# First tile of x in two halves with its norm weights beside it, first weight columns first on their queue, five warm-up matmuls for nine

## The chip, the cores and the metric

The kernel runs on one core of one Trainium2 chip. The metric is the device time of one execution in microseconds (us); the figure given for a kernel is the median of its runs. Before the change it is 734.75 us, the median of three runs that lie between 734.32 and 734.83.

## What is computed

One block of a hybrid model on 512 tokens of width 1024, in 32-bit floats. Each row of x is normalised (RMS) and scaled by g_mix, and one wide projection w_in makes the inputs of two branches, a gated linear attention in two directions and a latent attention with a rotary part. Their outputs are mixed by two sigmoid gates, projected by w_out and added to x. A feed-forward part with a squared ReLU and a last normalisation follow. Cut to what bears on this change:

```python
def reference(x, ...):
    n = rmsnorm(h, g_mix[l])          # x * rsqrt(mean(x*x) + EPS) * g_mix
    proj = n @ w_in[l]
    (gq, gk, gv, gr, z_gf, z_gb, cq, ckv, kr, z_ma, z_mb) = jnp.split(proj, SPLIT_IDX, axis=-1)
    y_gla = gla_branch(gq, gk, gv, gr, ...)
    y_mla = mla_branch(cq, ckv, kr, ...)
    merged = jax.nn.sigmoid(z_ma) * y_gla + jax.nn.sigmoid(z_mb) * y_mla
    h = h + merged @ w_out[l]
    m = rmsnorm(h, g_mlp[l])
    h = h + jnp.square(jax.nn.relu(m @ w_ff1[l])) @ w_ff2[l]
    return rmsnorm(h, g_final)
```

The change touches only the start of `n @ w_in`: the first 128 of the 1024 features of x, against the first 512 columns that the kernel wants of w_in.

## The kernel before

**Arithmetic.** x is handed in transposed (`xt`, features by tokens), so that it lies in eight tiles of 128 features by 512 tokens, k = 0 to 7. A 32-bit product is made of three products of a shorter format: each operand is split into a high part (a rounding copy) and a low part (what is left), and high by high, low by high and high by low are summed in PSUM. The factor 1/rms of a row is not known at the start; the products are made with x times g_mix alone, and 1/rms is multiplied in later.

**The start.** Four column groups of 128 (the query and key of head 0 and two groups of the gate z_mb) are gathered on the host into `w_first`, 1024 by 512. TensorE (PE) sums all four side by side in four PSUM banks, `f_accs[0]` to `f_accs[3]`: for each k three groups of four matmuls of 128x512 (`first_with(k)`), 12 per tile and 96 in all. In the trace the tiles of x are `x`, the loaded weights `vw`, the split x is `xT` (high part and low part in one tile), the split weights are `first0h`, `first0l` and so on (two k to a tile), and the banks are `first`.

**What feeds it.** SyncE (SP) issues the loads of x and of the weights in turn, tile by tile; ScalarE (ACT) issues two: `gvec`, which holds all norm weights and biases as columns (g_mix among them), and columns 128 to 511 of the first weight tile. Each engine works through its own list in order; a DMA that finds its turn of the eight completion counters still in use waits for the load eight places before it. For k = 0, VectorE (DVE) makes the high part of the weights in two casts (128 and 384 columns), ACT makes the high part of x (`ACTIVATE xT<-x,gvec`, scaled by the column of g_mix), and DVE then makes the two low parts. For k > 0 both high parts are ACT's. ACT also squares each tile of x for 1/rms.

**Before the data is there** PE runs nine matmuls of ones by ones into a bank of no use (`warm`). Each is in 32-bit floats and shows as two rows in the trace.

**What sets the order.** The start is written in program order, and each engine is held to it. From `nc.keep()` to `nc.flush((0.0, TABLES))` the rest of the kernel is collected and put in order by a planner (`Due`) from costs and due times that it works out itself.

Nearly every instruction passes through `Script.lay`, so that it shows as L233, and rows are told apart by their tiles. The loads stand at L732 to L741, the warm-ups at L745, `first_with` at L751, and the splitting of each tile at L768 to L784.

Of the kernel before, what the change touches and what calls it, by code (L numbers as in the profile page):

```python
# [13 lines left out]
F32R = mybir.dt.float32r  # L14
I32 = mybir.dt.int32
AF = mybir.ActivationFunctionType
ALU = mybir.AluOpType
AX = mybir.AxisListType

P = 128  # L20
S = 512
NT = S // P
D = 1024
KD = D // P
# [436 lines left out]
def tile_block(ctx: ExitStack, tc: tile.TileContext, t, out: bass.AP):  # L461
# [7 lines left out]
    bass_nc, nc = tc.nc, Script(tc.nc, issued_after)  # L469
# [5 lines left out]
    def tl(shape, dt, tag, bufs, name):  # L475
        serial[0] += 1
        name = f"{name}_{serial[0]}"
        return hold(lambda: sb.tile(shape, dt, tag=tag, bufs=bufs, name=name), shape, dt, tag, bufs, name)

    def hold(make, shape, dt, tag, bufs, name):  # L480
        h = Held(make, shape, dt, tag, bufs)
        h.name = name
        if nc.kept is None:
            nc.takes(h)
        return View.whole(h)

    def u2(name, dt=F32, shape=(P, S)):
        return tl(list(shape), dt, "u2", 24, name)

    def u4(name, dt=F32R, shape=(P, 2, S)):  # L490
        return tl(list(shape), dt, "u4", 30, name)
# [4 lines left out]
    def ps(tag, name):  # L496
        serial[0] += 1
        name = f"{name}_{serial[0]}"
        return hold(lambda: pp.tile([P, S], F32, tag=tag, bufs=4, name=name), [P, S], F32, tag, 4, name)

    def one(shape, dt, name):
        return hold(lambda: sb.tile(shape, dt, tag=name, bufs=1, name=name), shape, dt, name, None, name)

    def raw(x):
        return x.bitcast(F32)
# [6 lines left out]
    def split(hi, lo, src, rest=nc.vector):  # L512
        nc.scalar.activation(hi, src, AF.Copy)
        rest.tensor_tensor(lo, src, raw(hi), op=ALU.subtract)

    def split_scaled(hi, lo, src, scale):
        nc.scalar.activation(hi, src, AF.Copy, scale=scale)
        nc.vector.scalar_tensor_tensor(lo, src, scale, raw(hi), op0=ALU.mult, op1=ALU.subtract)

    def traced():  # L520
        return len(nc.cur_bb.bb.instructions)
# [25 lines left out]
    TABLES = {AF.Exp: 1, AF.Tanh: 1, AF.Ln: 2, AF.Sin: 3}  # L547
    V_GLA, V_Q, V_KV, V_MLP, V_BF, V_BB, V_MIX, V_CST = 0, 8, 11, 13, 21, 25, 29, 37
    gvec = one([P, 48], F32, "gvec")
    nc.scalar.dma_start(gvec[:, 0 : V_CST + 2], t["columns"])  # L550
    ident = one([P, P], F32, "ident")
    make_identity(bass_nc, ident.real())
    after = one([P, P], F32, "after")
# [4 lines left out]
    ones = one([P, P], F32, "ones")  # L558
    nc.vector.memset(ones, 1.0)
    ones_r = one([P, P], F32R, "ones_r")  # L560
    nc.vector.tensor_copy(ones_r, ones)
    half_pi = one([P, 1], F32, "half_pi")
    nc.gpsimd.memset(half_pi, float(np.pi / 2))
    mhalf = one([P, 1], F32, "mhalf")
# [5 lines left out]
    gmix, cst = gvec[:, V_MIX : V_MIX + 8], gvec[:, V_CST : V_CST + 2]  # L570
# [70 lines left out]
    def halves(nk, nw, name):  # L641
        wh = tl([P, nk, nw], F32R, "wh", 4, f"{name}h")
        wl = tl([P, nk, nw], F32R, "wl", 4, f"{name}l")
        return wh, wl
# [86 lines left out]
    xT = [u4(f"xT{k}") for k in range(KD)]  # L731
    xraw = [u2(f"x{k}") for k in range(KD)]  # L732
    vraw = [u2(f"vw{k}") for k in range(KD)]

    landing = traced()
    for k in range(KD):
        nc.sync.dma_start(xraw[k], t["xt"][k * P : (k + 1) * P, :])
        parts = ((nc.sync, slice(0, S)),) if k else ((nc.sync, slice(0, P)), (nc.scalar, slice(P, S)))
        for queue, c in parts:
            queue.dma_start(vraw[k][:, c], t["w_first"][k * P : (k + 1) * P, c])  # L740

    landing = landing, traced()
    fixed = traced()
    warm = ps("at", "warm")
    for _ in range(9):  # L745
        nc.tensor.matmul(warm[:, :P], ones, ones, start=True, stop=True)
    f_accs = [ps("mm", f"first{i}") for i in range(NT)]
    vh = [halves(2, S, f"first{k}") for k in range(KD // 2)]
    sq = None

    def first_with(k):  # L751
        hi, lo = xT[k][:, 0, :], xT[k][:, 1, :]
        wh, wl = vh[k // 2][0][:, k % 2, :], vh[k // 2][1][:, k % 2, :]
        for x, (a, b) in enumerate(((wh, hi), (wl, hi), (wh, lo))):
            for i in range(NT):
                nc.tensor.matmul(
                    f_accs[i], a[:, i * P : (i + 1) * P], b, start=k == 0 and x == 0, stop=k == KD - 1 and x == 2
                )

    def add_square(k, before):  # L760
        q = u2(f"sq{k}")
        nc.scalar.activation(q, xraw[k], AF.Square)
        if before is not None:
            nc.vector.tensor_tensor(q, q, before, op=ALU.add)
        return q

    for k in range(KD):
        wh, wl = (vh[k // 2][x][:, k % 2, :] for x in range(2))  # L768
        if k == 0:
            for c in (slice(0, P), slice(P, S)):  # L770
                nc.vector.tensor_copy(wh[:, c], vraw[k][:, c])
            hi, lo = xT[k][:, 0, :], xT[k][:, 1, :]
            nc.scalar.activation(hi, xraw[k], AF.Copy, scale=gmix[:, k : k + 1])
            nc.vector.tensor_tensor(wl, vraw[k], raw(wh), op=ALU.subtract)
            nc.vector.scalar_tensor_tensor(
                lo, xraw[k], gmix[:, k : k + 1], raw(hi), op0=ALU.mult, op1=ALU.subtract
            )
        else:
            split_scaled(xT[k][:, 0, :], xT[k][:, 1, :], xraw[k], gmix[:, k : k + 1])
            split(wh, wl, vraw[k])  # L780
        if k < 6:
            first_with(k)
        if k:
            sq = add_square(k - 1, sq)  # L784
# [7 lines left out]
    for k in range(KD):  # L792
        nc.scalar.activation(xraw[k], xraw[k], AF.Copy, scale=gmix[:, k : k + 1])
    first_with(6)
    first_with(7)
    x_diag = rstd_diag(x_tot, D, "x", False, zb_early[0][1])
    zb_early[1][1]()
# [953 lines left out]
    for n in range(4 * MH + LAG_C - 1):  # L1751
# [9 lines left out]
        b = n - LAG_B  # L1761
# [7 lines left out]
        for x, at in (("y", (18, 26, 34)), ("z", (20, 28, 36))):  # L1769
            if n in at:  # L1770
                p = at.index(n)
                to = (5, 6) if x == "y" else (7, 3)
                split_sum(wo_left[p], sums_of[p, x], *to, f"{x}o{p}", nc.gpsimd if p < 2 else nc.vector)
        if n in (19, 30):
            p = (19, 30).index(n)
# [17 lines left out]
        c = n - LAG_C  # L1793
# [702 lines left out]
def build(arrays):  # L2496
    nc = bacc.Bacc("TRN2", target_bir_lowering=False, num_devices=1, dynamic_dma_scratch_size=8192)
    t = {
        n: nc.dram_tensor(f"in_{n}", list(a.shape), mybir.dt.from_np(a.dtype), kind="ExternalInput").ap()
        for n, a in arrays.items()  # L2500
    }
    out = nc.dram_tensor("out_0", [1, S, D], F32, kind="ExternalOutput").ap()
    with tile.TileContext(nc) as tc:
        tile_block(tc, t, out)
    return nc
# [16 lines left out]
```

## Time and profile before

| What | Value |
|---|---|
| median of three runs | 734.75 us (734.32 to 734.83) |
| the profiled execution, first to last instruction (its span) | 733.0 us |
| mean granted TensorE clock of that execution | 0.998 |
| PE busy | 724.6 us, 99% of the span |
| PE weight loads busy | 635.9 us |
| DVE busy | 608.6 us |
| ACT busy | 515.8 us |
| GpSimd (POOL) busy | 199.8 us |

The profiled execution's own time is given as its span only; the median of the runs is 1.75 us above it. Times in the rows are microseconds from the start of the span. A row of the timeline has start, duration, engine, line, operation, output <- inputs, shapes and a count where like instructions in a row are merged; in square brackets stands how long the engine was idle before and what ended that. ACTq and SPq rows are the issuing of DMAs. Loads have a time from issue to landing of their own. The ends of matmuls are modelled, so their pace is read from start to start.

### The profile page before, as it was taken

To read this page: it belongs to the slowest core of one execution; us is meant where nothing else is said; L and a number is where in the kernel's file an instruction comes from. 1 tells how busy PE (TensorE), PEld (TensorE's weight loads), DVE (VectorE), ACT (ScalarE), POOL (GpSimd) and SP (SyncE) were. 2 spreads that over 40 slices of the span, in tenths; PEclk is the share of its full clock that TensorE was granted. 3 is DMA by queue.
4 is the path that set the end of the run, shared out by engine and by line. 5 is a ranking of instruction groups with operands and counts; after the bars stand their busy time and mean duration, and the time that the engine had idled before them with its cause. 6 is when DMAs were issued, how large, how long until landed. Compare 5 with 4: busy or idle time off the path is not lost.

```text
span 733.0 us, 11354 instructions
## 1 busy us (share of the span) xinstructions
PE 724.6 (99%) x4126; PEld 635.9 (87%) x4126; DVE 608.6 (83%) x960; ACT 515.8 (70%) x863; POOL 199.8 (27%) x207
## 2 busy tenths in 40 slices
PE   9999999999999999999999999999999999999996
PEld 8888888888899888888888999889988998889985
DVE  7694766669999789899998899968895789768885
ACT  8575665669998567998865788737864587458844
POOL 0133040401201215038843231321232212212433
PEclk9999999999999999999999999999999999999999
DMA  9979795742322224239996899898999888998973
GB/s 322 324 152 178 202 204 104 124 107 57 88 59 55 37 54 107 59 111 257 232 288 97 194 208 247 173 196 205 212 217 211 210 192 200 211 226 175 227 146 116
DMA packets 105306, 124.37 MB, mean 170 GB/s; under 512 B 16321, under 2 KB 68801, under 8 KB 105249
## 3 DMA queue, kind: packets, MB, share of 16 engines
q0 software_dynamic: 32992, 51.12, 41.3%
q1 hardware_dynamic: 71824, 72.04, 31.7%
q8 instruction: 32, 0.52, 0.3%
q10 hardware_dynamic: 432, 0.48, 0.2%
q14 instruction: 26, 0.20, 0.1%
HBM read 119.95 MB, written 2.10 MB: 167 GB/s over the span
## 4 chain that ended last, share of the span: by engine, by line
PE 99%; issue 0%; DVE 0%; ACT 0%; POOLq 0%; POOL 0%
PE mb L233 25%; PE ab L233 18%; PE zb L233 4%; PE first L233 3%; PE s L233 3%; PE av L233 3%; PE wox L233 3%; PE gvx L233 3%; PE zax L233 3%; PE grx L233 3%; PE cq L233 2%; PE gq L233 2%; PE gk L233 2%; PE tp L233 2%; PE uv L233 2%; PE ckv L233 1%
## 5 line engine op out<-in xcount | busy, mean ns | idle before, releaser
L233 POOL DMA_DIRECT2D ms<-in_w_ff x37 | 48.0, 1394 | 118.8 <-DVE hl0l L233 40.9
L233 POOL DMA_DIRECT2D w1s<-in_w_ff x19 | 24.3, 1277 | 85.5 <-DVE hl2l L233 25.8
L233 DVE TENSOR_TENSOR h<-h,ab 128x512 f32<-128x512 f32 x48 | 31.6, 681 | 8.4 <-PE ab L233 8.4
L233 ACT ACTIVATE row<-row 128x512 f32<-128x512 f32 x56 | 34.8, 623 | 1.2 <-DVE row L233 0.6
L233 PE MATMUL s<-kbuf,q 96*128 96x512 f32 x96 | 28.7, 409 | 0.0
L233 PE MATMUL av<-pT,v 128*128 128x512 f32 (+1 forms) x108 | 28.3, 383 | 0.0
L233 PE MATMUL mb<-four,hl0h 128*128 128x256 f32 x144 | 26.4, 283 | 0.0
L233 ACT ACTIVATE row<-mb 128x512 f32<-128x512 f32 x30 | 17.7, 589 | 9.5 <-PE mb L233 9.2
L233 ACT ACTIVATE e<-s,top 128x512 f32<-128x512 f32 x32 | 21.9, 685 | 3.4 <-DVE top L233 3.4
L233 PE MATMUL mb<-four,hl3h 128*128 128x256 f32 x128 | 23.5, 283 | 0.0
L233 DVE TENSOR_REDUCE top<-s 128x1 f32<-128x512 f32 x32 | 21.8, 683 | 1.7 <-PE s L233 1.5
L233 PEld LDWEIGHTS mb<-four,hl0h 128*128 128x128 f32 x144 | 22.8, 192 | 0.4
L233 DVE TENSOR_TENSOR pT<-tp,pT 128x512 fp32r<-128x512 f32 x32 | 21.7, 679 | 1.6 <-ACT pT L233 1.3
L233 ACT ACTIVATE pT<-tp 128x512 fp32r<-128x512 f32 x32 | 18.9, 595 | 2.9 <-PE tp L233 2.7
L233 PE MATMUL mb<-four,hl2h 128*128 128x256 f32 x112 | 20.5, 283 | 0.0
L233 PEld LDWEIGHTS mb<-four,hl3h 128*128 128x128 f32 x128 | 20.2, 192 | 0.3
L233 PE MATMUL mb<-four,hl0l 128*128 128x256 f32 x72 | 20.4, 283 | 0.0
L233 PE MATMUL tp<-ident,e 128*128 128x128 f32 x128 | 20.1, 273 | 0.0
L233 PEld LDWEIGHTS av<-pT,v 128*128 128x128 f32 x108 | 17.8, 189 | 2.6
L233 PEld LDWEIGHTS s<-kbuf,q 96*128 96x128 f32 x96 | 16.8, 189 | 3.4 <-ACT e L233 0.7
L233 ACT ACTIVATE hl3h<-ms 128x1024 fp32r<-128x1024 f32 x12 | 12.7, 1057 | 9.7 <-PE ab L233 4.6
L233 PEld LDWEIGHTS tp<-ident,e 128*128 128x128 f32 x128 | 15.8, 140 | 4.0 <-PE tp L233 0.2
(1122 smaller groups left out, 2789.0 us busy)
## 6 DMA issues: line engine op xcount, KB each, us to landing
ms<-in_w_ff POOLq DMA_DIRECT2D x37, 512.0 KB, 7.2
w1s<-in_w_ff POOLq DMA_DIRECT2D x19, 512.0 KB, 7.3
ms<-in_w_ff SPq DMA_DIRECT2D x16, 512.0 KB, 5.6
w1s<-in_w_ff SPq DMA_DIRECT2D x15, 512.0 KB, 6.0
wf0f<-in_w_ff SPq DMA_DIRECT2D x11, 512.0 KB, 6.5
wf1f<-in_w_ff SPq DMA_DIRECT2D x11, 512.0 KB, 5.9
wf2f<-in_w_ff SPq DMA_DIRECT2D x11, 512.0 KB, 6.2
w<-in_w_out POOLq DMA_DIRECT2D x10, 512.0 KB, 8.6
```

The costliest lines, as they stand in the source:

```text
L233: return call(*map(real, work.args), **{k: real(v) for k, v in work.named.items()})
```

## The change

Five edits, all at the start:

1. The first half (tokens 0 to 255) of the first tile of x comes as a new array `x_head`, 128 by 257, whose last column is g_mix of these 128 features. It is the first load on SP's queue. The second half is loaded into the tile of x by the second.
2. The first 128 weight columns move from SP's queue to the front of ACT's, ahead of the other 384; `gvec` goes behind both.
3. For k = 0 the high and the low part of x are each made in two halves, scaled by the column in `x_head` instead of the one in `gvec`. POOL copies the first half into the tile of x, where the squares read it.
4. The first matmul of the first bank becomes two of 256 tokens. So that both may add, the bank is first set by a matmul of `ones_r` with a tile of zeros (`nil`, made by DVE from `ones`).
5. Four matmuls of ones are left; with the one that sets the bank PE has five before the first real one.

The two new tiles come from the pool of 24 that x, weights and others share. The order on every engine behind the start is the same as before.

```diff
@@ -547,7 +547,6 @@
     TABLES = {AF.Exp: 1, AF.Tanh: 1, AF.Ln: 2, AF.Sin: 3}
     V_GLA, V_Q, V_KV, V_MLP, V_BF, V_BB, V_MIX, V_CST = 0, 8, 11, 13, 21, 25, 29, 37
     gvec = one([P, 48], F32, "gvec")
-    nc.scalar.dma_start(gvec[:, 0 : V_CST + 2], t["columns"])
     ident = one([P, P], F32, "ident")
     make_identity(bass_nc, ident.real())
     after = one([P, P], F32, "after")
@@ -559,6 +558,10 @@
     nc.vector.memset(ones, 1.0)
     ones_r = one([P, P], F32R, "ones_r")
     nc.vector.tensor_copy(ones_r, ones)
+    nil = u2("nil", F32R)
+    nc.vector.tensor_scalar(
+        nil.rearrange("p (a b) -> p a b", a=NT), ones.unsqueeze(1).to_broadcast([P, NT, P]), 0.0, None, op0=ALU.mult
+    )
     half_pi = one([P, 1], F32, "half_pi")
     nc.gpsimd.memset(half_pi, float(np.pi / 2))
     mhalf = one([P, 1], F32, "mhalf")
@@ -732,19 +735,26 @@
     xraw = [u2(f"x{k}") for k in range(KD)]
     vraw = [u2(f"vw{k}") for k in range(KD)]
 
+    HEAD = S // 2
+    x_head = u2("x_head")
     landing = traced()
-    for k in range(KD):
+    nc.scalar.dma_start(vraw[0][:, 0:P], t["w_first"][0:P, 0:P])
+    nc.sync.dma_start(x_head[:, 0 : HEAD + 1], t["x_head"])
+    nc.scalar.dma_start(vraw[0][:, P:S], t["w_first"][0:P, P:S])
+    nc.sync.dma_start(xraw[0][:, HEAD:S], t["xt"][0:P, HEAD:S])
+    nc.scalar.dma_start(gvec[:, 0 : V_CST + 2], t["columns"])
+    for k in range(1, KD):
         nc.sync.dma_start(xraw[k], t["xt"][k * P : (k + 1) * P, :])
-        parts = ((nc.sync, slice(0, S)),) if k else ((nc.sync, slice(0, P)), (nc.scalar, slice(P, S)))
-        for queue, c in parts:
-            queue.dma_start(vraw[k][:, c], t["w_first"][k * P : (k + 1) * P, c])
+        nc.sync.dma_start(vraw[k], t["w_first"][k * P : (k + 1) * P, :])
+    nc.gpsimd.tensor_copy(xraw[0][:, 0:HEAD], x_head[:, 0:HEAD])
 
     landing = landing, traced()
     fixed = traced()
     warm = ps("at", "warm")
-    for _ in range(9):
+    for _ in range(4):
         nc.tensor.matmul(warm[:, :P], ones, ones, start=True, stop=True)
     f_accs = [ps("mm", f"first{i}") for i in range(NT)]
+    nc.tensor.matmul(f_accs[0], ones_r, nil, start=True, stop=False)
     vh = [halves(2, S, f"first{k}") for k in range(KD // 2)]
     sq = None
 
@@ -752,7 +762,10 @@
         hi, lo = xT[k][:, 0, :], xT[k][:, 1, :]
         wh, wl = vh[k // 2][0][:, k % 2, :], vh[k // 2][1][:, k % 2, :]
         for x, (a, b) in enumerate(((wh, hi), (wl, hi), (wh, lo))):
-            for i in range(NT):
+            if k == x == 0:
+                for c in (slice(0, HEAD), slice(HEAD, S)):
+                    nc.tensor.matmul(f_accs[0][:, c], a[:, 0:P], b[:, c], start=False, stop=False)
+            for i in range(1 if k == x == 0 else 0, NT):
                 nc.tensor.matmul(
                     f_accs[i], a[:, i * P : (i + 1) * P], b, start=k == 0 and x == 0, stop=k == KD - 1 and x == 2
                 )
@@ -769,12 +782,13 @@
         if k == 0:
             for c in (slice(0, P), slice(P, S)):
                 nc.vector.tensor_copy(wh[:, c], vraw[k][:, c])
-            hi, lo = xT[k][:, 0, :], xT[k][:, 1, :]
-            nc.scalar.activation(hi, xraw[k], AF.Copy, scale=gmix[:, k : k + 1])
+            hi, lo, g = xT[k][:, 0, :], xT[k][:, 1, :], x_head[:, HEAD : HEAD + 1]
+            parts = (slice(0, HEAD), x_head[:, 0:HEAD]), (slice(HEAD, S), xraw[k][:, HEAD:S])
+            for c, src in parts:
+                nc.scalar.activation(hi[:, c], src, AF.Copy, scale=g)
             nc.vector.tensor_tensor(wl, vraw[k], raw(wh), op=ALU.subtract)
-            nc.vector.scalar_tensor_tensor(
-                lo, xraw[k], gmix[:, k : k + 1], raw(hi), op0=ALU.mult, op1=ALU.subtract
-            )
+            for c, src in parts:
+                nc.vector.scalar_tensor_tensor(lo[:, c], src, g, raw(hi[:, c]), op0=ALU.mult, op1=ALU.subtract)
         else:
             split_scaled(xT[k][:, 0, :], xT[k][:, 1, :], xraw[k], gmix[:, k : k + 1])
             split(wh, wl, vraw[k])
@@ -2514,6 +2528,9 @@
         np.concatenate([w[:, C_GQ : C_GQ + P], w[:, C_GK : C_GK + P], w[:, C_ZB : C_ZB + 2 * P]], axis=1)
     )
     arrays["xt"] = np.ascontiguousarray(arrays["x"][0].T)
+    arrays["x_head"] = np.ascontiguousarray(
+        np.concatenate([arrays["xt"][:P, : S // 2], arrays["columns"][:, 29:30]], axis=1)
+    )
     nc = build(arrays)
     res = bass_utils.run_bass_kernel_spmd(
         nc, [{f"in_{n}": a for n, a in arrays.items()}], core_ids=[0]
```

## Prediction, made before the result was known

> **What bounds the kernel now.** I read the chain of waits first, then what PE waited for, then the first ten microseconds engine by engine.
>
> ```profile
> PE 99%; issue 0%; DVE 0%; ACT 0%; POOLq 0%; POOL 0%
> ...
> PE warm L233 <- DVE ones L233: 1.1, 1, 1.1
> PE mb L233 <- ACT row L233: 0.5, 1, 0.5
> ```
>
> The chain that ended last is PE nearly throughout, and PE itself stood idle only 1.1 us at the start and 0.5 us in the last part. So a microsecond saved or lost on PE in the first tile goes straight to the end; nothing behind it has slack to give back or a load to wait for. PE's timeline at the start (start, duration, engine, line, operation):
>
> ```profile
> 1.11 3.91 PEld L233 LDWEIGHTS warm<-ones 128*128 128x128 f32 x18 [1.11 <-DVE ones L233]
> 4.97 1.93 PE L233 MATMUL first<-xT,first0h 128*128 128x512 f32 x4
> 5.54 1.36 PE L233 MATMUL first<-xT,first0h 128*128 128x512 f32 x3
> 5.97 0.93 PE L233 MATMUL first<-xT,first0h 128*128 128x512 f32 x2
> 6.39 0.51 PE L233 MATMUL first<-xT,first0h 128*128 128x512 f32 x1
> 6.74 1.08 PE L233 MATMUL first<-xT,first0l 128*128 128x512 f32 x4
> 6.97 0.85 PE L233 MATMUL first<-xT,first0l 128*128 128x512 f32 x3
> 7.20 0.62 PE L233 MATMUL first<-xT,first0l 128*128 128x512 f32 x2
> 7.66 1.98 PE L233 MATMUL first<-xT,first0h 128*128 128x512 f32 x8
> ```
>
> Two things are to be seen. The warm-up matmuls fill PE from 1.11 until the first real one, without a gap. And the pace changes: from start to start a 128x512 matmul takes 0.43 us until 6.39 (5.54, 5.97, 6.39) and 0.23 us from 6.74 on (6.74, 6.97, 7.20). PE works at about half pace until some 6.6 us, that is for 5.5 us after its first instruction.
>
> What the first real matmul waited for stands on ACT and DVE, and in the landing times of the loads:
>
> ```profile
> 0.80 0.41 ACTq L233 DMA_DIRECT2D gvec<-in_columns  x1
> 1.25 0.42 SPq L233 DMA_DIRECT2D vw<-in_w_first  x1
> 1.27 0.43 ACTq L233 DMA_DIRECT2D vw<-in_w_first  x1
> 3.93 0.72 ACT L233 ACTIVATE xT<-x,gvec 128x512 fp32r<-128x512 f32 x1 [1.41 <-DMA gvec<-in_columns]
> 5.22 0.72 ACT L233 ACTIVATE xT<-x,gvec 128x512 fp32r<-128x512 f32 x1 [0.57 <-DMA x<-in_xt]
> ...
> 4.12 0.23 DVE L233 CAST first0h<-vw 128x128 fp32r<-128x128 f32 x1 [2.81 <-DMA vw<-in_w_first]
> 4.48 0.36 DVE L233 CAST first0h<-vw 128x384 fp32r<-128x384 f32 x1
> ...
> x<-in_xt SPq DMA_DIRECT2D x1, 256.0 KB, 2.9
> gvec<-in_columns ACTq DMA_DIRECT2D x1, 19.5 KB, 3.1
> vw<-in_w_first ACTq DMA_DIRECT2D x1, 192.0 KB, 3.2
> vw<-in_w_first SPq DMA_DIRECT2D x1, 64.0 KB, 2.9
> ```
>
> The x tile lands at 0.80 + 2.9 = 3.70, gvec at 3.90, and ACT starts at 3.93: gvec came last. ACT ends at 4.65, the second cast at 4.84. The warm-ups ran a little past both, so the data held PE back by nothing, and the warm-ups by some 0.1 to 0.2 us.
>
> **The change part by part.** On PE the stream starts like this, before and now (`first_27` to `first_30` before, `first_29` to `first_32` now, are the four banks; `first0h` the high part of the weights):
>
> ```order
> L233 MATMUL warm_125<-ones 128x128 x9
> L233 MATMUL first_27_135<-xT_2_84,first0h_139 128x512
> L233 MATMUL first_28_136<-xT_2_84,first0h_139 128x512
> L233 MATMUL first_29_137<-xT_2_84,first0h_139 128x512
> L233 MATMUL first_30_138<-xT_2_84,first0h_139 128x512
> ```
>
> ```order
> L233 MATMUL warm_130<-ones 128x128 x4
> L233 MATMUL first_29_135<-nil_74,ones_r 128x512
> L233 MATMUL first_29_135<-xT_3_85,first0h_140 128x256 x2
> L233 MATMUL first_30_136<-xT_3_85,first0h_140 128x512
> L233 MATMUL first_31_137<-xT_3_85,first0h_140 128x512
> L233 MATMUL first_32_138<-xT_3_85,first0h_140 128x512
> ```
>
> Five warm-ups went, one 512-wide setter came, and the first real matmul is two. On ACT's list, before and now (`vw_18`, now `vw_19`, is the first weight tile, `x_10`, now `x_11`, the first tile of x):
>
> ```order
> L233 DMA gvec<-in_columns 128x39
> L567 ACT_TABLE_LOAD
> L233 DMA vw_18_100<-in_w_first 128x384
> L233 ACTIVATE xT_2_84<-x_10_92,gvec 128x512
> L233 ACTIVATE xT_3_85<-x_11_93,gvec 128x512
> ```
>
> ```order
> L570 ACT_TABLE_LOAD
> L233 DMA vw_19_101<-in_w_first 128x128
> L233 DMA vw_19_101<-in_w_first 128x384
> L233 DMA gvec<-in_columns 128x39
> L233 ACTIVATE xT_3_85<-x_head_109 128x256
> L233 ACTIVATE xT_3_85<-x_11_93,x_head_109 128x256
> L233 ACTIVATE xT_4_86<-x_12_94,gvec 128x512
> ```
>
> gvec moved from first to third, and is first needed by the second tile of x.
>
> *When PE falls idle.* 18 warm-up rows take 3.91 us, 0.217 each; eight take 1.74 and end at 2.85. The setter is a 512-wide matmul at the slow pace, 0.43: PE is through at 3.28. Its zeros come from one DVE instruction of 128x512 behind 1.32; the nearest such row lasts 0.66, so they are there by 2.0.
>
> ```profile
> L233 DVE TENSOR_SCALAR e<-e,tot 128x512 f32<-128x512 f32 x16 | 10.6, 660 | 0.1
> L233 ACT ACTIVATE four<-row 128x256 fp32r<-128x256 f32 x18 | 7.3, 413 | 0.4
> L233 POOL TENSOR_TENSOR wk2l<-wk2f,wk2h 128x256 fp32r<-128x256 f32 x2 | 1.4, 735 | 0.0
> 1.80:2.20 0.40, 0.40 (x4) 0.40 (x4) 0.00 (x0) 0.40 (x1) 0.01 (x1) 1.00 0.60 82
> 2.60:3.00 0.40, 0.40 (x4) 0.40 (x4) 0.00 (x0) 0.00 (x0) 0.00 (x0) 1.00 1.00 352
> ```
>
> *When the first half is ready.* The loads move their first bytes at about 1.8 and reach 352 GB/s (last number of the two stretches) by 2.6. Ahead of ACT's start stood 256 + 19.5 KB; now it is 128.5 KB of x_head and 64 KB of weights beside it. 83 KB less at 352 GB/s is 0.24 us: x_head lands at about 3.46 (no later than gvec's 3.90). ACT's half takes 0.41 by the 128x256 row, and from ACT's end at 4.65 to the first weight load behind it was at most 0.25; I take 0.2. The first half matmul starts at 4.1 and lasts 0.21.
>
> *When PE runs without a break again.* The second half of x is second on SP's queue, where the 64 KB of weights were; these landed at 1.25 + 2.9 = 4.15. It is 64 KB larger, 0.18 us: 4.33. Bounds: 4.15, and 4.47, where the 192 KB landed. With 0.41 on ACT and 0.2 behind it the second half matmul starts at 4.94 and ends at 5.15. The other 384 columns stay second on ACT's queue: 4.47, plus 0.36, plus 0.2 is 5.03, just covered. So the second bank's matmul starts at 5.15, where it started at 5.54: 0.39 us earlier (0.25 to 0.50 by the bounds).
>
> *What that is worth.* These 0.39 us lie in the slow stretch. If the pace rises at the same moment, 6.6, PE has done 0.39/0.43 = 0.91 matmuls more by then, and each saves 0.23 later: 0.21 us.
>
> *What the pause costs.* This is the unknown. PE, unbroken before, is idle from 3.28 to 4.94 but for 0.21: 1.45 us. Each microsecond by which the pace rises later costs 1 - 0.23/0.43 = 0.465 us. Lower bound: the rise doesn't care, 0. Upper bound: the 5.5 us start anew at 4.94, the rise comes at 10.4 instead of 6.6, and 3.8 us cost 1.77. The end of the program shows the nearest row on pauses:
>
> ```profile
> 725.88 0.28 PE L233 MATMUL mb<-hl3h,four 128*128 128x256 f32 x1
> ...
> 725.00:733.00 8.00, 1.16 (x10) 0.95 (x8) 2.38 (x7) 2.62 (x7) 1.10 (x2) 0.83 0.53 198
> 730.30:733.00 2.70, 0.00 (x0) 0.00 (x0) 0.00 (x0) 0.00 (x0) 0.00 (x0) 0.50 0.30 112
> ```
>
> The granted clock there (0.83 over 8 us, 0.50 at the end) fell at about 730.3, 4.1 us after PE's last matmul at 726.2. So the gate takes microseconds to notice idleness, and pauses of 0.6 and 0.8 us shouldn't throw away what was gathered: not the upper end. But it needed 5.5 us of work, so idle time isn't free either. I take the middle case, that the rise comes later by the idle time itself: 1.45 x 0.465 = 0.67 us.
>
> The Trainium skill, "TensorE: Matmul & The Clock Gate", Part 1, says that the clock rises after a window of some 3.4 us that was busy, and that the windows run free of the program. By that rule a spoiled window puts the rise off by 3.41 us at once, 1.59 us, and the sum would be 736.1 instead of 735.2. The trace agrees with its half and full pace (0.43 and 0.23), but shows one rise alone, which can't tell how busy is enough.
>
> *Costed at nothing.* The two halves on ACT are 0.1 us longer than one whole; ACT's next work, the second tile of x, starts only when that lands, 5.22. gvec, issued third at about 1.75, lands 3.1 later at 4.85, ahead of the same 5.22; if it came later, the second tile would have until about 8 us. DVE's casts end at 4.84 as before, the low weights by 5.5, wanted by PE after four matmuls at 6.4, and the two low halves of x by 6.5, wanted at 7.4 at the earliest. POOL's copy of the first half (0.74 by the nearest 128x256 row) ends by 4.3; the first square wants it at 6.9. On SP the loads behind keep their places, one counter earlier in the round; the third tile's weights may go out half a microsecond later, against 2.7 us of cover:
>
> ```profile
> 6.87 0.61 ACT L233 ACTIVATE sq<-x 128x512 f32<-128x512 f32 x1
> ...
> 8.00 0.62 ACT L233 ACTIVATE first1h<-vw 128x512 fp32r<-128x512 f32 x1
> ...
> 11.28 1.07 PE L233 MATMUL first<-xT,first1h 128*128 128x512 f32 x4
> ```
>
> **The sum.** 733.0 - 0.21 + 0.67 = 733.5 us of span. The median of the runs lies 1.75 above the profiled span, so 735.2. What a measurement of this kernel can tell from no change is about 0.2%, 1.47 us: faster is below 733.28, slower above 736.22. The forecast is no change.
>
> **The rivals.** First, the rise comes at the same moment, pause or not: 734.75 - 0.21 = 734.5. For it: the slow fall at the end. Against: nothing before 6.6 counted at once.
>
> Second, the other side: the pause spoils the rise. The gathered work is lost, the 5.5 us run from 4.94, and the time is 734.75 - 0.21 + 1.77 = 736.3. It shows as slower once the rise is more than (1.47 + 0.21)/0.465 = 3.6 us later. For it: up to 3.2 us PE had been busy for 2.1 us, and that didn't bring the rise; in the 3.3 us from there to 6.6 it would now be busy for about 1.9, where it was busy throughout. Against: the slow fall.
>
> Third, all of the front comes sooner: the rest of x and of the weights lands by 3.8, since less stands ahead of it, the second bank starts at 4.5, and the rise moves along. 1.04 us: 733.7. Against: the 192 KB row landed 3.2 us after its issue, and its place isn't better.
>
> Fourth, the change doesn't do what it says: the second half of x lands as late as 4.7 behind the loads beside it, the second bank starts at 5.5 as before, the pause grows by 0.36: 734.75 + 1.81 x 0.465 = 735.6.
>
> **How the numbers follow.** Forecast 0.37, first rival 0.28, second 0.23, third 0.07, fourth 0.05. Faster: half of the third, 0.04. Slower: half of the second, whose time lies at the mark, and a little of the forecast, 0.16. The same: 0.80. The range reaches from 733.9, below the first rival with the better bound of the loads, to 736.5, above the second: the third is left out.
>
> **What would show it.** Right: an idle stretch of PE after the setter of about 0.8 us and one of 0.6 behind the first half matmul; the second bank's matmul near 5.15; the change from 0.43 to 0.23 near 8 us; the rest of PE's timeline moved as a whole by the same amount. The first rival shows as a pace change at 6.6, the second near 10. What would make it wrong: x_head landing later than 3.9, a second bank behind 5.5, or a new wait of PE in the second tile.

## The result, and the profile after

The changed kernel takes 739.23 us (median of five runs, 738.31 to 739.95), against 734.32 us for the kernel before beside it (733.67 to 734.83). The ratio is 1.0066, with an interval of 1.0056 to 1.0077: slower, by 4.9 us. The profiled execution spans 737.8 us where it was 733.0; its own time was 739.54.

What bounds the kernel is still PE. The shares of the chain, from the page of the changed kernel:

```profile
PE 98%; DMA 0%; issue 0%; DVE 0%; ACT 0%; POOLq 0%; POOL 0%; SPq 0%
```

And what PE waited for (total, times, longest, in us):

```profile
PE warm L233 <- DVE ones L233: 1.1, 1, 1.1
PE mb L233 <- ACT row L233: 0.5, 1, 0.5
PE first L233 <- DVE first0h L233: 0.2, 1, 0.2
PE first L233 <- ACT xT L233: 0.2, 1, 0.2
```

Only the last two are new, and they come to 0.4 us. The other 4.4 us are no wait at all. PE's start in the changed kernel:

```profile
2.84 0.77 PE L233 MATMUL first<-nil,ones_r 128*128 128x512 f32 x1
3.83 0.55 PE L233 MATMUL first<-xT,first0h 128*128 128x256 f32 x1 [0.21 <-DVE first0h L233]
4.55 1.86 PE L233 MATMUL first<-xT,first0h 128*128 128x256 f32 x4 [0.17 <-ACT xT L233]
4.93 1.49 PE L233 MATMUL first<-xT,first0h 128*128 128x512 f32 x3
6.21 1.91 PE L233 MATMUL first<-xT,first0l 128*128 128x512 f32 x4
7.92 3.13 PE L233 MATMUL first<-xT,first0h 128*128 128x512 f32 x8
10.88 1.07 PE L233 MATMUL first<-xT,first0l 128*128 128x512 f32 x4
11.80 1.07 PE L233 MATMUL first<-xT,first0h 128*128 128x512 f32 x4
```

The data came sooner: the second bank's matmul starts at 4.93 (the row that holds the last three of the four above it), 0.61 us before its old 5.54. But four matmuls take 1.71 us from 6.21 to 7.92, still the slow 0.43 each, and 0.92 from 10.88 to 11.80, the quick 0.23. The eight between take 2.96: some 5.6 slow and 2.4 quick, so the pace rises at 7.92 + 5.6 x 0.43 = 10.3 us, where it rose at 6.6. The trace's record of the granted clock has its first entry at 10.34, and at 6.63 before.

The rest shows in the chain of waits, whose pieces have start, length and number of matmuls. The kernel before:

```profile
29.18 10.92 PE zb L233 x48
...
380.27 5.44 PE woz L233 x24
...
474.37 10.91 PE ab L233 x48
...
628.57 10.91 PE ab L233 x48
```

The changed kernel, the same pieces:

```profile
30.59 10.92 PE zb L233 x48
...
381.80 5.62 PE woz L233 x24
...
476.74 11.24 PE ab L233 x48
...
632.24 11.24 PE ab L233 x48
```

The first lies 1.41 us later, the second 1.53, the third 2.37, the last 3.67. So the front lost 1.41, and nearly all of the rest is lost far from every edited line, from 380 us on. `zb` takes 10.92 in both; `woz` went from 5.44 to 5.62 and `ab` from 10.91 to 11.24, that is from 0.227 to 0.234 us a matmul. There are the same instructions in the same order, and no waits. What differs is where their operands lie. Read from the built programs, the start in bytes of each pool in a partition:

```
pool                           before    after    remainder by 512
24 tiles (nil, x, gh, gl..)     10720    10560    480, now 320
next pool up                    59872    59872    480, 480
split weights (hl, bo..)       182752   182752    480, 480
matmuls 128x512 with the stationary operand in the pool of 24 (gh, gl)
and the moving one in a split-weight tile (hl, bo): 480; from start
to start, read for 465 of them, 227.1 ns, now 234.1
```

A pool is laid down where its first tile is taken. `nil` is taken ahead of five tiles of 32 bytes (`half_pi`, `mhalf` and the three of `r_x`), so the pool of 24 slid down by 160 bytes past them; the pools above stayed. The 480 matmuls at 7 ns more are 3.36 us: with the front's 1.41 that is 4.77 of the 4.8.

Last, ACT's start and the loads of the changed kernel (KB, us from issue to landing):

```profile
1.74 0.45 ACTq L233 DMA_DIRECT2D gvec<-in_columns  x1
3.17 0.51 ACT L233 ACTIVATE xT<-x_head 128x256 fp32r<-128x256 f32 x1 [1.09 <-DMA x_head<-in_x_head]
3.99 0.51 ACT L233 ACTIVATE xT<-x,x_head 128x256 fp32r<-128x256 f32 x1 [0.31 <-DMA x<-in_xt]
7.04 0.72 ACT L233 ACTIVATE xT<-x,gvec 128x512 fp32r<-128x512 f32 x1 [2.54 <-DMA gvec<-in_columns]
```

```profile
x_head<-in_x_head SPq DMA_DIRECT2D x1, 128.5 KB, 2.3
x<-in_xt SPq DMA_DIRECT2D x1, 128.0 KB, 2.7
...
x<-in_xt SPq DMA_DIRECT2D x1, 256.0 KB, 4.9
gvec<-in_columns ACTq DMA_DIRECT2D x1, 19.5 KB, 5.2
```

x_head was there by 3.17 and the second half by 3.99. gvec landed 5.2 us after its issue, near 7.0, and ACT stood for 2.54 us. But gvec was not the only late one: the second tile of x (the row of 256 KB, issued at 1.71) landed 4.9 us after its issue, near 6.6, where the same load took 3.5 before the change. Of ACT's idle time only the last 0.3 to 0.4 us are gvec's.

### The profile page after: what moved, and what is told of

It reads as the page before. It is cut to its first block, busy times and chain, and to the rows that moved or that the text cites. A ratio compares the mean times of both kernels' runs of the same rounds, so it can differ in the third digit from the quotient of the medians.

```text
span 737.8 us, 11343 instructions
## 1 busy us (share of the span) xinstructions
PE 729.1 (99%) x4118; PEld 636.0 (86%) x4118; DVE 610.4 (83%) x962; ACT 516.0 (70%) x864; POOL 200.2 (27%) x208
## 4 chain that ended last, share of the span: by engine, by line
PE 98%; DMA 0%; issue 0%; DVE 0%; ACT 0%; POOLq 0%; POOL 0%; SPq 0%
PE mb L233 25%; PE ab L233 19%; PE zb L233 4%; PE first L233 3%; PE s L233 3%; PE av L233 3%; PE wox L233 3%; PE gvx L233 3%; PE zax L233 3%; PE grx L233 3%; PE cq L233 2%; PE gk L233 2%; PE gq L233 2%; PE tp L233 2%; PE uv L233 2%; PE woz L233 2%
```

## The experiments

Two theories had to be told apart for each part: for the later stages the address of the pool, or anything else that the front passes on; for the front the pause in PE, or the halves and the moved loads.

**The pool back in its place: `late_nil`.** The changed kernel, with `nil` taken behind the first old tile of the pool:

```diff
-    nil = u2("nil", F32R)
-    nc.vector.tensor_scalar(
...
     half_pi = one([P, 1], F32, "half_pi")
...
     R = u2("R")
+    nil = u2("nil", F32R)
+    nc.vector.tensor_scalar(
...
```

> The changed kernel with the tile of zeros taken from its pool behind the small tiles instead of ahead of them, so that the pool of 24 begins at byte 10720 of a partition as before, not at 10560; every instruction is the same. Theory A (the address of the pool makes the 465 matmuls with a stationary operand from it 7 ns slower each): 3.3 of the 4.9 us go, 1.4 us of the front stay, some 735.9 us, and those matmuls are back at 227 ns. Theory B (the later loss comes from which buffer the tiles fall into, two places on in the round, or from the late front): the time stays near 739 and the matmuls at 234 ns.

Measured: 735.46 us (12 runs, 734.75 to 736.42) beside 734.39 before; ratio 1.0013, interval 1.0004 to 1.0021. The chain of this run:

```profile
29.91 10.92 PE zb L233 x48
...
381.93 5.44 PE woz L233 x24
...
476.01 10.91 PE ab L233 x48
```

`woz` and `ab` are back at their old lengths, the matmuls of the table at 227.2 ns. The loss in the late stages goes with the place of `nil`'s allocation.

This chain is 0.73 us later than before at `zb` and 1.66 at `woz`, though. Between them lies a wait of PE that no other of the fourteen profiles has; PE's row from the list of waits, and a pair of small instructions on DVE, here and in the kernel before:

```profile
PE y L233 <- ACT l L233: 0.8, 1, 0.8
```

```profile
199.20 1.12 DVE L233 TENSOR_TENSOR c3f<-e3f 128x1 f32<-128x1 f32 x2
```

```profile
198.48 0.22 DVE L233 TENSOR_TENSOR c3f<-e3f 128x1 f32<-128x1 f32 x2
```

The profile names ACT, but the matmul that waits reads `gra`, which DVE began at 202.28 here and at 200.59 before, and it starts 0.62 us behind that in both. DVE was late because its pair took 0.9 us longer, while POOL worked on `qsb` (199.29 to 200.30); in the other profiles the pair took 0.22 or 0.23, and it was POOL's next instruction that was longer, 1.99 or 2.00 for 1.00. So 0.73 us of this execution are the front's and 0.93 are not. It is one of the slower runs of this kernel (736.37); whether the others had the same wait is not recorded.

**The address alone: `pool_first`.** The kernel before, with only the allocation of `R`, the pool's first tile, moved; no instruction changes.

```diff
+    R = u2("R")
     half_pi = one([P, 1], F32, "half_pi")
...
     r_x, x_var, x_eps = (one([P, NT], F32, f"r_x{i}") for i in range(3))
-    R = u2("R")
```

> The kernel before with one line moved: the tile R is taken from the pool of 24 ahead of the five small tiles, so that the pool begins at byte 10560; the instructions and which buffer each tile gets are the same. Theory A (address): slower by 465 x 7 ns = 3.3 us, some 737.6, matmuls with a stationary operand of the pool at 234 ns, front as before. Theory B (buffers or a late front): no change, 734.3.

Measured: 737.52 us (five runs, 737.29 to 738.28) beside 734.39; ratio 1.0042, interval 1.003 to 1.0054. With nothing else touched, 160 bytes cost 3.1 us; the matmuls take 234.1 ns, as in the changed kernel. This settles the larger part.

**What about the address: `shift32` to `shift512`, and `all32`.** Each is the kernel before with the allocations moved: `R` goes ahead of one, two, three or four of the small tiles (the pool 32, 64, 96 or 128 bytes lower), or ahead of `ones_r` with the small tiles put before it (512 lower). `all32` puts an unused tile of 32 bytes ahead of everything, so that all pools move together.

```diff
-    r_x, x_var, x_eps = (one([P, NT], F32, f"r_x{i}") for i in range(3))
+    r_x, x_var = (one([P, NT], F32, f"r_x{i}") for i in range(2))
     R = u2("R")
+    x_eps = one([P, NT], F32, "r_x2")
```

That was `shift32`; and `all32`:

```diff
+    pad = one([P, 8], F32, "pad")
     gvec = one([P, 48], F32, "gvec")
```

> The kernel before with the tile R taken from the pool of 24 ahead of one of the five small tiles only: the pool begins 32 bytes lower (byte 10688), everything else lies where it lay. Theory A1 (the stationary operand must lie in the same phase of 64 bytes as the moving one): 32 is half of 64, so slow as with 160: 234 ns, 737.5 us. Theory A2 (phase of 512 bytes, each step away costs more): between 227 and 234 ns, some 735 us. Theory A3 (any difference costs the same): 234 ns. If 227 ns and 734.4 us: 32 bytes do no harm.

> As the kernel before it, with the pool 64 bytes lower (byte 10656). Theory A1 (phase of 64 bytes): 227 ns and 734.4 us, no loss. Theory A2 and A3: slower than before, 230 to 234 ns, 735.5 to 737.5 us.

> The kernel before with the pool 96 bytes lower (R ahead of three of the small tiles), an odd multiple of 32. By what 0, 32, 64 and 160 bytes gave (227, 234, 229, 234 ns): 233 to 234 ns if the phase of 64 bytes is what counts; between 229 and 234 if the cost grows with the distance.

> The kernel before with the pool 128 bytes lower, an even multiple of 64. If the phase of 128 bytes is free: 227 ns. If every multiple of 64 but 0 costs a little: 229 ns. If the cost grows with the distance: 232 ns or more.

> The kernel before with the pool 512 bytes lower (R ahead of the 512-byte tile ones_r, the five small tiles left ahead of it), everything else in its place. If only the phase of 512 bytes counts: 227 ns and 734.4 us, as with no shift. If the cost grows with the distance in bytes whatever the phase: 232 ns or more and 736.5 us or more.

> The kernel before with an unused tile of 32 bytes ahead of all others, so that every tile lies 32 bytes higher and the big pools begin at multiples of 512; the distance between stationary and moving operands is the same as before. Theory A1 as a matter of distance: 227 ns and 734.4 us. As a matter of the stationary operand's own place (a multiple of 64 is bad): 234 ns for nearly all of the 1950 matmuls of 512 columns, and some 10 us or more slower.

Measured (the kernel before stood at 734.39 to 734.54 beside them; ns is the mean from start to start, over 465 of the 480 matmuls):

```
kernel       pool by  ns     median us       ratio (interval)
shift32      -32      233.2  737.59          1.0039 (1.0024 to 1.0054)
shift64      -64      229.0  735.63          1.0018 (1.0009 to 1.0027)
shift96      -96      233.4  737.24, one run
shift128     -128     232.4  736.95, one run
pool_first   -160     234.1  737.52          1.0042 (1.0030 to 1.0054)
shift512     -512     227.1  734.79          1.0005 (0.9995 to 1.0015)
all32        all +32  227.1  734.08          0.9996 (0.9987 to 1.0005)
```

The piece of 48 matmuls near 474 us in the chain, for -64, -128 and all +32, one run in each fence:

```profile
474.03 10.99 PE ab L233 x48
```

```profile
474.66 11.15 PE ab L233 x48
```

```profile
473.47 10.91 PE ab L233 x48
```

Moving everything by 32 bytes costs nothing, moving one pool by 32 costs 6 ns a matmul: it is the distance between the two operands that counts, not the place of either. A distance changed by 512 is as good as none, 64 costs 2 ns and 128 costs 5; so a rule of multiples of 64 falls. A rule by the remainder of the distance by 512 fits all seven, and so does one by the remainder by 256. Of the distances between 128 and 512 only 160 was tried, and why a distance matters is open.

**The pause alone: `five_only`.** The kernel before with five matmuls of ones:

```diff
-    for _ in range(9):
+    for _ in range(5):
         nc.tensor.matmul(warm[:, :P], ones, ones, start=True, stop=True)
```

> The kernel before with five matmuls of ones instead of nine and nothing else changed: PE pauses from about 3.3 to 4.9 us. If a pause spoils a whole step of the clock: the pace changes near 10 us and the time rises by 1.4 to 1.7 us, 735.9. If idle time only puts the rise off by itself: plus 0.7, 735.0. If the pause doesn't matter: 734.3.

Measured: 736.02 us (11 runs, 735.29 to 736.55) beside 734.39; ratio 1.0016, interval 1.0008 to 1.0025. PE's start in this run:

```profile
1.11 2.50 PE L233 MATMUL warm<-ones 128*128 128x128 f32 x10 [1.11 <-DVE ones L233]
4.69 2.07 PE L233 MATMUL first<-xT,first0h 128*128 128x512 f32 x4 [1.08 <-ACT xT L233]
6.57 1.78 PE L233 MATMUL first<-xT,first0l 128*128 128x512 f32 x4
8.19 2.00 PE L233 MATMUL first<-xT,first0h 128*128 128x512 f32 x8
```

The first real matmul starts 0.28 us earlier than before (4.69 for 4.97), and yet the kernel is slower: four matmuls still take 1.62 from 6.57 to 8.19, so the pace rises near 8.1. Four fewer warm-ups by themselves cost time. How much is less sure: the medians are 1.63 us apart, the interval of the ratio allows 0.6 to 1.8 us, and the execution shown is the quickest of the eleven, with a span (733.6 us) only 0.6 above that of before.

**The halves without a pause: `late_nil_nine` and `late_nil_eight`.** `late_nil` with eight or seven matmuls of ones and the one that sets the bank:

```diff
-    for _ in range(4):
+    for _ in range(8):
```

(and `range(7)` in the second)

> As the first kernel, with nine matmuls ahead of the first real one again (eight of ones and the one that sets the bank), so that PE has no pause. Theory A with the pause as the cause of the late clock: the pace changes as early as in the kernel before, 5 to 7 us, and the time is that of before less 0.2 us, 734.1. If the halves and the moved loads themselves cost the front its 1.4 us (the late gvec, the smaller loads): 735.9, like the first kernel.

> The changed kernel with the pool at its old place and seven matmuls of ones, so that with the one that sets the bank PE is busy until about 4.4 us and has no pause longer than 0.2 us before the first tile. If the pause was the only harm of the front: the second bank's matmul at 5.0, the pace changes where it does without a pause, and the time is that of before less 0.2 us, 734.2. If the late second tile of x (landing 6.6 us instead of 5.2) now holds PE: an idle stretch near 8 us and 734.4 or more.

Measured: 734.45 (11 runs), ratio 1.0004 (0.9996 to 1.0013), and 734.23 (11 runs), ratio 1.0001 (0.9993 to 1.001). With PE kept busy and the pool in place, all the rest of the change is worth nothing that can be told from noise, neither a gain nor a loss. In `late_nil_eight` the late loads come to light:

```profile
6.61 1.08 PE L233 MATMUL first<-xT,first0h 128*128 128x512 f32 x4
7.97 1.19 PE L233 MATMUL first<-xT,first0h 128*128 128x512 f32 x4 [0.28 <-ACT first0h L233]
```

The pace had risen early here (at 4.32), PE was through the first tile by 7.7 and stood 0.28 us for the second, whose split ACT began only at 6.67, when gvec had landed. The tile itself had landed only 0.3 us before that, near 6.4, 4.7 us after its issue at 1.71.

**gvec ahead of the 384 columns: `eight_gvec`.** `late_nil_eight` with gvec second on ACT's queue:

```diff
+    nc.scalar.dma_start(gvec[:, 0 : V_CST + 2], t["columns"])
     nc.scalar.dma_start(vraw[0][:, P:S], t["w_first"][0:P, P:S])
     nc.sync.dma_start(xraw[0][:, HEAD:S], t["xt"][0:P, HEAD:S])
-    nc.scalar.dma_start(gvec[:, 0 : V_CST + 2], t["columns"])
```

> The changed kernel with the pool at its old place, eight matmuls ahead of the first real one, and gvec issued second on ACT's queue, ahead of the other 384 weight columns. If gvec's late landing was what held the second tile: ACT starts on it at the landing of that tile of x, PE's idle stretch of 0.28 us near 8 us goes, some 734.0 us; the 384 columns land up to 0.3 us later, which may cost as much at the second bank. No more than 0.3 us either way.

Measured: 737.44 us (six runs, 735.83 to 739.32) beside 734.46; ratio 1.0043, interval 1.0031 to 1.0056. Loads, then PE's and DVE's start:

```profile
vw<-in_w_first ACTq DMA_DIRECT2D x1, 192.0 KB, 4.9
...
gvec<-in_columns ACTq DMA_DIRECT2D x1, 19.5 KB, 2.6
```

```profile
7.10 1.65 PE L233 MATMUL first<-xT,first0h 128*128 128x512 f32 x3 [1.78 <-DVE first0h L233]
...
6.69 0.36 DVE L233 CAST first0h<-vw 128x384 fp32r<-128x384 f32 x1 [2.95 <-DMA vw<-in_w_first]
```

gvec is early now (2.6 us), and the 384 columns take its place: 4.9 us as third where they took 3.0 as second. PE stands 1.78 us for them, and its pace rises at 10.21. So the lateness goes with being third on that queue, not with what is loaded. And gvec was not what held the second tile: third on SP's queue, that tile landed 4.8 us after its issue here too. What makes the third loads of both queues late is open; before the change, with two loads on ACT's queue, SP's third took 3.5.

**When the pace rises**, by the first entry of the record of the granted clock, in us of the span, and how long it stayed up:

```
without a pause of PE                    rise    up for
before                                   6.63    723.63
shift32, 64, 96, 128, 512                6.89, 5.20, 5.30, 5.78, 7.05
pool_first, all32                        4.93, 4.79
late_nil_nine, late_nil_eight            6.09, 4.32
with one
five_only                                8.07    723.63
late_nil                                 8.81    723.63
eight_gvec                              10.21    723.63
after                                   10.34    723.63
```

Ten profiles without a pause lie between 4.3 and 7.1, four with one between 8.1 and 10.3; the means, 5.7 and 9.4, are 3.7 apart, while single pairs lie from 1.0 to 6.0 apart. In ten of the fourteen the clock stays up for 723.63 us, in four for 727.04: two values 3.41 apart, though the program ends at different times. The clock is thus changed on a beat of 3.41 us, which the program does not set. The Trainium skill, "TensorE: Matmul & The Clock Gate", Part 1, gives windows of about 3.4 us that run free of the program; the trace agrees, 723.63 / 212 and 727.04 / 213 both being 3.413.

On this beat the window before the rise of the changed kernel's clock began at 6.93, when PE had no more gaps; the one before that, from 3.51 to 6.93, held the two pauses and did not count. They were 0.38 us by the rows' brackets, and 0.8 if the matmuls ahead of them are taken as 0.43 and 0.21 long. In `eight_gvec` the window from 6.80 to 10.21 did count, with PE idle until 7.10. How busy a window has to be lies between these two, and was not measured closer. Where a window begins is not set by the program, so the size of the loss in one execution is in part chance.

## Why the prediction was wrong

**The step that failed most** is the one in which everything behind the first tile is left alone: "the rest of PE's timeline moved as a whole by the same amount". It moved by 1.41 us and then grew to 3.67 by 632 us. The prediction asked of `nil` and `x_head` only what work makes them, and never where they lie. The pool of 24 slid by 160 bytes, 480 matmuls became 7 ns longer, and 3.36 us were missing from the sum; no rival had them. `late_nil` and `pool_first` show it from both sides. The profile of before held no row that prices this, and instructions listed in order cannot show it, since they don't change.

**The pause.** The middle case, a rise later by the idle time itself, was mis-sized: it forecast a net loss of 0.46 us (0.67 less the 0.21 of the earlier start) where the profiled execution lost 1.41. The pauses themselves, forecast at 0.8 and 0.6, were shorter: 0.56 and 0.51 if the matmuls ahead are taken at the slow pace. Yet the rise came at 10.34, 3.71 us later. At 0.465 each these cost 1.73; the start 0.61 earlier gives back 0.61 / 0.43 x 0.23 = 0.33; 1.40 is left, and the chain shows 1.41. This is the second rival's sign ("near 10"). Its reason as first told, that the gathered 5.5 us of work are lost, is not quite the one shown: what is lost is the window that holds the pause. The prediction's sentence on the Trainium skill ("TensorE: Matmul & The Clock Gate", Part 1) had this mechanism, with 1.59 us; `five_only` measured 1.63 between medians, with room for 0.6 to 1.8, so that the two figures lie this close is luck. The slow fall at the end, on which the middle case leaned, spoke of how windows turn the clock down and not of what turns it up. Yet `late_nil`, the change without the address, has a median only 1.07 above before, in two groups of runs (734.75 to 735.11 and 735.8 to 736.4). In its profiled execution, of the upper group, the front lost only 0.73 us and a wait near 200 us the rest; what the other runs lost where is not recorded. By its median alone the middle case, with 735.2, would stand: that a lost window is the mechanism rests on the times of the rises, not on this total.

**When the data is ready** was right in direction and cautious in size: the first half starts at 3.83 (forecast 4.1), the second at 4.55 (4.94), the second bank at 4.93 (5.15, with 5.04 as the better bound). That the gain in the slow stretch is small fits too: `late_nil_nine` and `late_nil_eight`, which have it without a pause, can't be told from before, and a gain of 0.21 is too small for these runs to show.

**Costed at nothing**: gvec was forecast for 4.85 and landed near 7.0, and the second tile of x, taken to land at 5.22 as before, landed near 6.6. gvec's 3.1 us were taken from a row where it was first on its queue. PE had no wait for the second tile here, being still slow; in `late_nil_eight`, with PE quick, the two late loads together cost 0.28 us. The fallback that the prediction named, "about 8 us", is the point where PE stood. POOL's copy, low halves and SP's later loads made no wait of PE.

**The reading of what bounds the kernel** held: PE without slack, so that each lost piece of it went through to the end.

## What to carry to other kernels

A new tile in a shared pool can move the pool, and with it the operands of matmuls that the change never mentions: compare the addresses of the built programs as well as their instructions, and take a new tile behind the old ones. When a slowdown is spread over stages that were not edited, compare the length of equal pieces of the chain; a longer mean without a wait points to operands and not to order. Warm-up work on PE is to be cut only as far as the real work follows without a gap, since gaps that add up to less than a microsecond can put the full pace off by a whole window.

## What the runs showed of the hardware that was not expected

- A 128x512 matmul took 227 ns or up to 234, depending on the distance in a partition between its stationary operand and its moving one: -32 bytes 233.2, -64 229.0, -96 233.4, -128 232.4, -160 234.1, -512 227.1, and both moved together 227.1.
- The clock went up and down on a beat of 3.41 us that the program did not set (723.63 or 727.04 us apart in fourteen profiles), and a window with 0.4 to 0.8 us of idle PE did not bring it up.
- At the start, the third load on ACT's queue landed late, 19.5 KB and 192 KB alike: 5.2 us after its issue in the changed kernel, 4.4 in `late_nil_nine`, 4.8 in `late_nil_eight` and 4.9, with the 384 columns third, in `eight_gvec`; as second, the same loads took 2.6 and 3.0. The third load on SP's queue was late in the same profiles: 4.9, 4.2, 4.7 and 4.8, where it took 3.5 before the change.
- In one of fourteen profiles two small DVE instructions took 1.12 us instead of 0.22 while POOL worked on `qsb`, and PE lost 0.9 us by it.
